# A hybrid MLA and RWKV-7 layer with a PEER mixture on one core: which token blocks go through every expert and which gather, and 32 expert tiles' first products moved beside the mixers

## The chip, the cores and the metric

The kernel runs on one core of a Trainium2 chip. The metric is the device time of one execution in microseconds (us), lower is better. The engines are PE (TensorE; PEld is its weight load, which overlaps the matmuls), DVE (VectorE), ACT (ScalarE), POOL (GpSimd) and SP (SyncE, which issues most of the DMAs). Each engine works off its own instructions in a fixed order.

## The reference

512 tokens, model width 1024, all float32. Two mixers read the normed tokens, and a product-key expert layer follows. Cut to its core:

```python
h = rms_norm(x, g_mix);  p = h @ w_in
y_a = mla_group(p[..., :672], ...)      # latent attention, 8 heads, causal by chunks of 64
y_b = rwkv7_group(p[..., 672:], ...)    # RWKV-7, 8 heads, a state carried over the tokens
x = x + concat([y_a, y_b]) @ w_o
# PEER on h = rms_norm(x, g_ffn), 16384 experts of one neuron each
q = (h @ w_pq).reshape(T, 8, 2, 128)
s = einsum('thpd,hpnd->thpn', q, sub_keys)           # 128 scores per half key
s1, i1 = top_k(s[:, :, 0], 16);  s2, i2 = top_k(s[:, :, 1], 16)
top_s, pos = top_k(s1[..., :, None] + s2[..., None, :], 16)
idx = take(i1 * 128 + i2, pos);  gate = softmax(top_s)   # 8 heads x 16 = 128 experts a token
act = gelu(einsum('thkd,td->thk', expert_u[idx], h))
x = x + einsum('thk,thkd->td', gate * act, expert_v[idx])
```

## The kernel before

The tokens are four blocks of 128 (block 0 to 3). Work on them is written as generators that run in lanes: `front` (norm and the input columns of RWKV), `chunks` (RWKV within chunks), `latent` (the whole attention group), `scan` (RWKV's state), and one lane `back`, which holds the output projection, the second norm, the retrieval (queries against keys, top 16) and the routing (indices and gates). A loop at the end of the kernel picks the lane that is furthest behind in a table of costs; a scheduler of the framework then fixes the order of each engine's instructions. Lanes have pools of their own for SBUF and PSUM; the back lane has two PSUM banks.

The expert layer is done in two ways:

- **Gathered blocks** (`GATHERED`, `experts`): POOL fetches for each of the 128 (head, rank) pairs the rows of `expert_u` that the 128 tokens want, 128x1024 float32 by an indirect DMA into a tile `ga` (four buffers). DVE takes the product with the block's `h2` (one SCALAR_TENSOR_TENSOR and a read of its accumulator). The rows of `expert_v` are fetched likewise and added into `acc` by a second SCALAR_TENSOR_TENSOR. A block is 256 gathers of 512 KB, two blocks are 512. They can begin when the block's routing has written `idx`.
- **Dense blocks** (`DENSE`, `dense`): two blocks go through all 16384 experts, in 128 tiles of 128 experts. `gate_half` spreads the two blocks' gates over the experts (DVE makes B, ACT makes A, PE multiplies). `up(e)` multiplies a tile of `expert_ut` with the tokens: whole in float32, or split into two float32r halves by ACT and DVE (`split`) and three cheaper products on PE. `down(e)` multiplies the result with the gates on DVE and then with a tile of `expert_v`, whole or split, into four PSUM banks `po`. `u_whole` and `v_split` say which tile is done how. A few tiles' results (`KEPT`) are made early and wait in DRAM.

Before, block 0 and block 3 are gathered, and blocks 1 and 2 are dense; the back lane takes block 0 alone, then 1 and 2 together, then 3.

Of the kernel before, what the change touches and what calls it, by code (L numbers as in the profile page):

```python
# [8 lines left out]
F32 = mybir.dt.float32  # L9
# [47 lines left out]

LANE = {"R": 1, "M": 2, "S": 4, "F": 3, "B": 3}
# [4 lines left out]
PM = 7  # L63
BACK = [("F", (0,)), ("F", (1,)), ("B", (0,)), ("B", (1, 2)), ("B", (3,))]

GATHERED = (0, 3)
DENSE = (1, 2)
EARLY = 1
GROUP, GA = 32, 4


HALF, SUB, GBUFS = 64, 16, 5
FIRST, AHEAD, KEPT = 12, 16, 12
VB, SPB, XB, UCUT = 2, 2, 4, 2
# [3 lines left out]
def u_whole(e):  # L78

    return e < 28 or 47 <= e - AHEAD < 64  # L80

# [6 lines left out]
def layer_kernel(ctx: ExitStack, tc: tile.TileContext, x, pos, cvec, rvec, w_mla, w_rwkv, w_uq, w_ukv, lora, g2,  # L88
# [46 lines left out]
    def cst(shape, name, dt=F32, pool=pre):  # L135
        return pool.tile(shape, dt, name=name)
# [200 lines left out]
    def rwkv_in(b, hT):  # L337
        pm = {}
        if b == EARLY:

            t = [gb([P, D], "ga", GA).rearrange("p (a b) -> p a b", b=P) for _ in range(2)]
            pm = {"k": t[0][:, 0:4], "r": t[0][:, 4:8], "v": t[1][:, 0:4], "x": t[1][:, 4:6]}
        for g, cols in (("x", (12, 13)), ("k", range(4, 8)), ("r", range(4)), ("v", range(8, 12))):
            if b != EARLY:
                pm[g] = sb([P, 4, P], "pm", PM, pool=wa) if len(cols) == 4 else sb([P, 2, P], "px", 2, pool=wa)
# [508 lines left out]
    def route(b, tv, ti):  # L854
# [100 lines left out]
        o = DENSE.index(b) * P  # L955
        if not slots:
            slots.extend(pools[2].tile([P, nd], F32, tag="vs_2", name=f"slots{j}", bufs=3) for j in range(3))
        for j, dst in enumerate(slots):
            act(dst[:, o:o + P], p[:, j * P:(j + 1) * P], AF.Copy)

# [49 lines left out]

    def back(bs):
# [4 lines left out]
        lists = yield from retrieve(bs, h2T)  # L1016
        for b, (tv, ti) in zip(bs, lists):
            routed[b] = yield from route(b, tv, ti)

    def gate_half(dn, g, parts):  # L1020
# [23 lines left out]
    def dense():  # L1044
# [13 lines left out]
        def halves(shape, tag, bufs, pool=None, one=False):  # L1058
            cnt[0] += 1
            return [(pool or d2).tile(shape, F32R, tag=tag if one else tag + n, name=f"{tag}{n}{cnt[0]}", bufs=bufs)  # L1060
                for n in "hl"]

        hd = []
        for i in range(0, KC, 2):
# [15 lines left out]

        kept = {}
# [64 lines left out]
        n = nd // 8  # L1146
        rest = AHEAD - FIRST + KEPT
        for e in range(FIRST):
            up(e)
        for i, _ in enumerate(gate_half(dn, 0, [whole])):  # L1150
            for e in range(FIRST + i * rest // n, FIRST + (i + 1) * rest // n):
                up(e, e >= AHEAD)
        po = [[psd.tile([P, 512], F32, tag="po", name=f"po{i}{n}", bufs=2 * nt) for n in range(2)] for i in range(nt)]
# [26 lines left out]
    after = {"F": lambda b: [("R", b - 2), ("F", b - 1)] + ([("S", 0)] if b == 1 else []),  # L1180
             "R": lambda b: [("F", b)], "M": lambda b: [("F", b)],
             "S": lambda b: [("R", b)], "B": lambda b: [("S", b), ("M", b)]}
    lanes = [[("R", (b,)) for b in range(NB)], [("M", (b,)) for b in range(NB)], [("S", (b,)) for b in range(NB)],
             [(n, bs) for n, bs in BACK], [("F", (b,)) for b in range(2, NB)]]

# [3 lines left out]
    while any(lanes):  # L1189
# [15 lines left out]
        if running[i] is None:  # L1205
            running[i] = fn(bs) if n == "B" else fn(*bs)
            at[i] = t
# [71 lines left out]
```

## Time and profile before

| | |
|---|---|
| Median of 3 runs | 1789.32 us (1785.22 to 1790.51) |
| The profiled execution | 1786.83 us, of which its instructions span 1784.9 us |
| Busy share of the span | PE 91%, PE weight loads 76%, DVE 76%, ACT 51%, POOL 41% |
| Mean granted TensorE clock | 0.942 of full speed |
| Moved by DMA | 520.84 MB, a mean of 292 GB/s |

A busy share is the share of the span in which at least one instruction of the engine ran. Matmuls are pipelined, so that the busy share of PE counts their latency too. A difference of more than about 0.3% of the time can be told from none.

### The profile page before, as it was taken

The page shows a single profiled execution, that of the slowest core. Times are in us where ns is not written, and L with a number is a line of the kernel's source. Part 1 is how long each engine was busy: PE and PEld are TensorE (multiplying, and loading weights), DVE is VectorE, ACT ScalarE, POOL GpSimd, SP SyncE. Part 2 cuts the span into 40 slices and gives each one's busy share as a digit, 9 for nine tenths or more (in the row PEclk, how much of TensorE's full clock was granted, in tenths as well). Part 3 has the DMA queues.
Part 4 walks back from the last instruction along what each step waited for, and adds up shares of the span by engine and source line. Part 5 has one row for each costly group of instructions (what it writes and reads, how often), then busy time and mean ns, then how long its engine had stood idle before and what let it go on. Part 6 is the DMA issues. An engine that isn't in the chain of part 4 may idle for free. (4 is left out here: it accounts for less than half of the span.)

```text
span 1784.9 us, 31084 instructions
## 1 busy us (share of the span) xinstructions
PE 1622.3 (91%) x11143; PEld 1363.3 (76%) x11143; DVE 1352.8 (76%) x3010; ACT 907.3 (51%) x2421; POOL 723.1 (41%) x560
## 2 busy tenths in 40 slices
PE   7999998998879995789997799999989889999998
PEld 6896898877665784667995478888867778888876
DVE  3422446667775698987889789999878799999895
ACT  5645635444422622257766234444777735444444
POOL 1001100447664433555445343544555554447430
PEclk9999997995769998998998999999989999999999
DMA  8545643898789998889997799999889889999985
GB/s 276 187 139 191 237 163 111 322 313 268 262 272 329 318 313 305 287 297 331 376 328 244 284 363 355 330 348 340 313 318 324 310 306 355 373 340 333 354 280 177
DMA packets 154875, 520.84 MB, mean 292 GB/s; under 512 B 17313, under 2 KB 24097, under 8 KB 154721
## 3 DMA queue, kind: packets, MB, share of 16 engines
q0 software_dynamic: 73728, 268.47, 43.1%
q1 hardware_dynamic: 80992, 250.39, 39.3%
q8 instruction: 88, 1.44, 0.3%
q14 instruction: 67, 0.54, 0.1%
HBM read 508.96 MB, written 9.83 MB: 291 GB/s over the span
## 5 line engine op out<-in xcount | busy, mean ns | idle before, releaser
L970 POOL DMA_INDIRECT ga<-in_expert_v_dram,idx x256 | 359.0, 1402 | 366.7 <-DVE acc L983 260.9
L970 POOL DMA_INDIRECT ga<-in_expert_u_dram,idx x256 | 311.9, 1218 | 337.7 <-DVE ga L980 234.2
L983 DVE SCALAR_TENSOR_TENSOR acc<-ga,dots,acc 128x1024 f32<-128x1024 f32 x256 | 327.6, 1280 | 63.7 <-DMA ga<-in_expert_v_dram,idx 60.8
L980 DVE SCALAR_TENSOR_TENSOR ga<-ga,h 128x1024 f32<-128x1024 f32 x256 | 311.6, 1219 | 65.0 <-DMA ga<-in_expert_u_dram,idx 62.1
L1141 PE MATMUL po<-xh,t 128*128 128x512 f32 x880 | 305.2, 406 | 11.7 <-DVE t L1056 5.6
L1109 PE MATMUL ps<-dh,ul 128*128 128x256 f32 x664 | 192.7, 290 | 10.6 <-DVE ul L1056 10.0
L1055 ACT ACTIVATE xh<-v 128x512 fp32r<-128x512 f32 x220 | 136.4, 627 | 121.5 <-PE po L1141 99.7
L1109 PE MATMUL ps<-dh,uh 128*128 128x256 f32 x664 | 189.7, 286 | 6.7 <-ACT uh L1055 5.2
L1141 PEld LDWEIGHTS po<-xh,t 128*128 128x128 f32 x880 | 160.9, 192 | 44.4 <-DVE t L1056 6.8
L1141 PE MATMUL po<-xl,t 128*128 128x512 f32 x440 | 179.2, 408 | 11.1 <-DVE xl L1056 10.4
L1109 PE MATMUL ps<-dl,uh 128*128 128x256 f32 x664 | 188.7, 284 | 0.0
L1095 PE MATMUL ps<-t,u 128*128 128x256 f32 x720 | 172.5, 392 | 12.8 <-DMA u<-in_expert_ut_dram 11.1
L1056 DVE TENSOR_TENSOR xl<-v,xh 128x512 fp32r<-128x512 f32 x220 | 149.6, 688 | 36.6 <-ACT xh L1055 34.1
L1095 PEld LDWEIGHTS ps<-t,u 128*128 128x128 f32 x720 | 138.6, 197 | 36.8 <-issue 6.6
L1031 ACT ACTIVATE A<-iotap,slots 128x128 f32<-128x128 f32 x512 | 156.2, 394 | 0.0
L1035 PEld LDWEIGHTS ps<-B,A 128*128 128x128 f32 x1024 | 128.8, 200 | 23.2 <-ACT A L1032 11.9
L1109 PEld LDWEIGHTS ps<-dh,ul 128*128 128x128 f32 x664 | 127.3, 192 | 21.8 <-DVE ul L1056 16.5
L1055 ACT ACTIVATE uh<-u 128x512 fp32r<-128x512 f32 x166 | 99.7, 626 | 86.3 <-PE ps L1109 67.6
L1109 PEld LDWEIGHTS ps<-dh,uh 128*128 128x128 f32 x664 | 127.4, 192 | 16.7 <-ACT uh L1055 8.0
L1035 PE MATMUL ps<-B,A 128*128 128x64 f32 x1024 | 128.5, 281 | 10.6 <-ACT A L1032 9.4
L1109 PEld LDWEIGHTS ps<-dl,uh 128*128 128x128 f32 x664 | 127.3, 192 | 3.0 <-issue 0.2
L840 PE MATMUL ps<-h2T,wst 128*128 128x128 f32 (+1 forms) x768 | 123.5, 315 | 1.6 <-DMA wst<-in_w_pq_dram 1.6
(391 smaller groups left out, 2845.7 us busy)
## 6 DMA issues: line engine op xcount, KB each, us to landing
u<-in_expert_ut_dram SPq DMA_DIRECT2D x128, 512.0 KB
v<-in_expert_v_dram SPq DMA_DIRECT2D x128, 512.0 KB
wst<-in_w_rwkv_dram SPq DMA_DIRECT2D x56, 512.0 KB
wst<-in_w_pq_dram SPq DMA_DIRECT2D x48, 512.0 KB
wst<-in_w_o_dram SPq DMA_DIRECT2D x24, 512.0 KB
wst<-in_w_mla_dram SPq DMA_DIRECT2D x16, 336.0 KB
t<-in_x_dram SPq DMA_DIRECT2D x8, 512.0 KB
wst<-in_w_ukv_dram SPq DMA_DIRECT2D x16, 256.0 KB
```

What stands on the lines that cost most here:

```text
L840: mm(p[:, :nb * P], w[:, kc, :], h2T[:, kc, :], start=kc == 0, stop=kc == KC - 1)
L970: G.indirect_dma_start(out=t, out_offset=None, in_=table, in_offset=bass.IndirectOffsetOnAxis(ap=idx[:, j:j + 1], axis=0))
L980: V.scalar_tensor_tensor(u, u, 1.0, h2, op0=OP.mult, op1=OP.mult, accum_out=dots[:, j:j + 1])
L983: V.scalar_tensor_tensor(acc, row_of(expert_v, j), dots[:, j:j + 1], acc, op0=OP.mult, op1=OP.add)
L1031: act(A[:, j, :], iotap, AF.Abs, scale=-1.0, bias=i2T[:, t0 + j:t0 + j + 1])
L1035: mm(p[:, j * HALF:(j + 1) * HALF], A[:, j, :], B[:, j, :], start=True, stop=True)
L1055: act(hi, t, AF.Copy)
L1056: V.tensor_tensor(lo, t, hi, op=OP.subtract)
L1095: mm(p, u[:, kc, :], hd[kc // 2][:, kc % 2, :], start=kc == 0, stop=kc == KC - 1)
L1109: mm(p, a[:, k, :], h[:, kc, :], start=kc + i == 0, stop=kc == KC - 1 and i == 2)
L1141: mm(po[i][n], ww[:, i * P:(i + 1) * P], vv, start=e + k == 0, stop=e == P - 1 and k == 2)
```

## The change

Blocks 0 and 1 become the dense pair, blocks 2 and 3 are gathered. The back lane is cut in two steps, `join` (output projection and norm) and `query` (retrieval and routing), and takes 0 and 1 together, then 2, then 3. A new lane `beside` starts when blocks 0 and 1 are joined: it reads their normed tokens back from DRAM, multiplies the first 32 tiles of `expert_ut` with them, whole, and writes the 32 results to DRAM; its PSUM is the back lane's two banks. `up(e)` of these tiles later loads the result and applies the gelu alone. Of the tiles after those, 16 instead of 12 are made ahead and kept in DRAM, and `u_whole` now holds for e < 48, so that 20 tiles fewer are split. The indices and gates of the dense blocks wait in DRAM (`slotd`). Tiles for the inputs of RWKV are shared with the `ga` buffers in two blocks instead of one.

```diff
-BACK = [("F", (0,)), ("F", (1,)), ("B", (0,)), ("B", (1, 2)), ("B", (3,))]
-
-GATHERED = (0, 3)
-DENSE = (1, 2)
-EARLY = 1
+PM = 3
+BACK = [("F", (0,)), ("F", (1,)), ("N", (0, 1)), ("Q", (0, 1)), ("N", (2,)), ("Q", (2,)), ("N", (3,)), ("Q", (3,))]
+
+GATHERED = (2, 3)
+DENSE = (0, 1)
+
+EARLY = (1, 2)
+
+BESIDE = 32
...
-FIRST, AHEAD, KEPT = 12, 16, 12
+FIRST, AHEAD, KEPT = 12, 16, 16
...
-    return e < 28 or 47 <= e - AHEAD < 64
+    return e < BESIDE + KEPT or 47 <= e - AHEAD < 64
...
+    def beside(_):
+
+        hd = ux.tile([P, KC, nd], F32, name="hdx")
+        nc.sync.dma_start(hd, h2d)
+        for e in range(BESIDE):
+            u = ux.tile([P, KC, P], F32, tag="ux", name=f"ux{e}", bufs=2)
+            nc.sync.dma_start(u, expert_ut[e])
+            p = bank()[:, :nd]
+            for kc in range(KC):
+                mm(p, u[:, kc, :], hd[:, kc, :], start=kc == 0, stop=kc == KC - 1)
+            t = ux.tile([P, nd], F32, tag="uy", name=f"uy{e}", bufs=2)
+            act(t, p, AF.Copy)
+            kept[e] = dp.tile([P, nd], F32, name=f"a{e}")
+            nc.sync.dma_start(kept[e], t)
+            yield
...
             if e in kept:
                 acts[e] = act_tile(e)
                 nc.sync.dma_start(acts[e], kept[e])
+                if e < BESIDE:
+                    act(acts[e], acts[e], AF.Gelu)
                 return
...
     stages = {"F": (front, 16, 32), "R": (chunks, 24, 110), "M": (latent, 46, 95), "S": (scan, 10, 28),
-              "B": (back, 42, 95)}
...
+              "N": (join, 11, 28), "Q": (query, 31, 67), "U": (beside, BESIDE, 8 * BESIDE)}
```

**Where the gathers begin.** On DVE, before, the first product of a gathered row (L980) stands at row 376 of 2062, among the mixers of blocks 2 and 3:

```order
L583 TENSOR_TENSOR pm_1792<-pm_1792,t_3862 128x512
L597 TENSOR_TENSOR pm_1915<-pm_1915,pm_1792 128x512
L980 SCALAR_TENSOR_TENSOR ga_15350,dots_15349<-ga_15350,h_15347 128x1024
L577 TENSOR_TENSOR t_3675<-t_3675,ps_3786 128x512
L353 SCALAR_TENSOR_TENSOR px_3479<-ps_3528,cv,px_3479 128x128
L353 SCALAR_TENSOR_TENSOR pm_3545<-ps_3548,cv,pm_3545 128x128
L748 TENSOR_TENSOR ST_164<-t_3794,ps_3789 64x4x64 x2
```

Of the change the first one (now L984) stands at row 688 of 1971, behind the routing of block 2 (L922):

```order
L922 SCALAR_TENSOR_TENSOR t_6677<-pi_6620,dl_6566 128x128 x7
L953 TENSOR_TENSOR gate_6810<-ge_6804,gs_6807 128x128
L922 SCALAR_TENSOR_TENSOR t_6677<-pi_6620,dl_6566 128x128 x2
L922 SCALAR_TENSOR_TENSOR t_6677<-bf_6695,dl_6566 128x128 x16
L984 SCALAR_TENSOR_TENSOR ga_15054,dots_15053<-ga_15054,h_15051 128x1024
L984 SCALAR_TENSOR_TENSOR ga_15057,dots_15053<-ga_15057,h_15051 128x1024
```

Before, 169 of the 512 products stand ahead of the dense stage's first DVE instruction; now 42 do, and none of the 512 stands ahead of an instruction of RWKV or attention.

**Where they end.** Before, the last products of gathered rows (L983) stand among the splits of the last dense tiles (L1056), and the row of the dense output (L1173) is last on DVE:

```order
L1056 TENSOR_TENSOR xl_14936<-v_14919,xh_14935 128x512
L983 SCALAR_TENSOR_TENSOR acc_16127<-ga_16902,dots_16131,acc_16127 128x1024
L1056 TENSOR_TENSOR t_15052<-wst_14293,t_15052 128x256
L1056 TENSOR_TENSOR xl_14952<-v_14945,xh_14951 128x512
L983 SCALAR_TENSOR_TENSOR acc_16127<-ga_16905,dots_16131,acc_16127 128x1024
L1056 TENSOR_TENSOR xl_14962<-v_14945,xh_14961 128x512
...
L1056 TENSOR_TENSOR xl_15326<-v_15309,xh_15325 128x512
L1173 TENSOR_TENSOR xx_15335<-xx_15335,po_8318 128x512
```

Of the change the last split (now L1081) stands at row 1861, and 102 products of gathered rows (L984, L987) stand behind it:

```order
L1081 TENSOR_TENSOR xl_15020<-v_15013,xh_15019 128x512
L1081 TENSOR_TENSOR xl_15030<-v_15013,xh_15029 128x512
L984 SCALAR_TENSOR_TENSOR ga_16302,dots_15835<-ga_16302,h_15833 128x1024
L1202 TENSOR_TENSOR xx_15039<-xx_15039,po_8706 128x512
L1202 TENSOR_TENSOR xx_15039<-xx_15039,po_8707 128x512
L987 SCALAR_TENSOR_TENSOR acc_15831<-ga_16305,dots_15835,acc_15831 128x1024
...
L987 SCALAR_TENSOR_TENSOR acc_15831<-ga_16537,dots_15835,acc_15831 128x1024
```

The gathers moved from both sides of the dense stage's start to its whole length and past its end.

**Where the 32 tiles stand.** On PE, before, the queries of blocks 1 and 2 (L840, against `w_pq`) stand between matmuls of block 3's attention (L482 to L499):

```order
L493 MATMUL ps_5136<-ident,t_5086 128x128 x4
L840 MATMUL ps_5984<-h2T_5293,wst_5982 128x256 x8
L499 MATMUL ps_5157<-vs_5073,t_5141 128x64
...
L840 MATMUL ps_6017<-h2T_5293,wst_6015 128x256 x6
L493 MATMUL ps_5210<-ident,t_5128 128x128 x4
```

Of the change the queries of block 2 (now L845) stand between tiles of `beside` (L1038) and the last steps of the scan (L727 to L778):

```order
L845 MATMUL ps_6118<-h2T_5840,wst_6116 128x128 x8
L1038 MATMUL ps_6130<-hdx,ux_6128 128x256 x8
L727 MATMUL ps_6926<-t_6924,t_6801 64x64 x3
...
L1038 MATMUL ps_6408<-hdx,ux_6406 128x256 x8
L845 MATMUL ps_6423<-h2T_5840,wst_6421 128x128 x8
L778 MATMUL ps_7004<-sg_5688,wst_7002 128x128
```

Behind the last query matmul of block 2 no attention is left; 19 of the 32 tiles stand ahead of that matmul, 24 ahead of the end of block 2's routing.

## Rows read from the trace of the kernel before

**Rows 1.** The page's first part: engine, busy us, share of the span, instructions.

```profile
PE 1622.3 (91%) x11143; PEld 1363.3 (76%) x11143; DVE 1352.8 (76%) x3010; ACT 907.3 (51%) x2421; POOL 723.1 (41%) x560
```

**Rows 2.** The chain that ended last, its longest piece: start, us, what.

```profile
1737.32 37.45 PE po L1141 x159
```

**Rows 3.** Four stretches: us; PE, PEld, DVE, ACT, POOL busy; granted clock; DMA share; GB/s.

```profile
0.00:319.00 319.00, 299.67 (x2895) 256.51 (x2896) 127.68 (x548) 172.40 (x554) 23.82 (x29) 0.97 0.56 185
319.00:700.00 381.00, 337.84 (x2589) 275.97 (x2587) 280.77 (x609) 155.52 (x496) 199.68 (x168) 0.87 0.88 305
700.00:1010.00 310.00, 259.04 (x1508) 216.95 (x1509) 270.73 (x812) 173.95 (x452) 149.19 (x111) 0.91 0.86 303
1010.00:1738.00 728.00, 685.96 (x3987) 582.27 (x3986) 649.39 (x1004) 385.58 (x884) 350.45 (x255) 0.98 0.93 334
```

**Rows 4.** Single lines: durations ns min/median/max, first and last start in us.

```profile
L952 ACT ACTIVATE idx<-ps x2: 278/278/278, 318.2 to 1004.4; 128x128 int32<-128x128 f32 x2
L840 PE MATMUL ps<-h2T,wst x256: 274/275/377, 213.2 to 279.1; 128*128 128x128 f32 x128
L840 PE MATMUL ps<-h2T,wst x256: 377/379/483, 603.0 to 691.5; 128*128 128x256 f32 x128
L840 PE MATMUL ps<-h2T,wst x256: 273/275/423, 844.8 to 928.8; 128*128 128x128 f32 x128
L499 PE MATMUL ps<-t,t x64: 221/275/421, 85.0 to 697.5; 128*128 128x64 f32 x64
```

**Rows 5.** PE by time, 859 to 864 us: one whole tile, and what follows it.

```profile
859.69 3.67 PE L1095 MATMUL ps<-t,u 128*128 128x256 f32 x16
863.20 0.38 PE L847 MATMUL ps<-wst,t 128*128 128x128 f32 x2
```

**Rows 6.** Groups of instructions: busy us, mean ns of one, then idle time before.

```profile
L983 DVE SCALAR_TENSOR_TENSOR acc<-ga,dots,acc 128x1024 f32<-128x1024 f32 x256 | 327.6, 1280 | 63.7 <-DMA ga<-in_expert_v_dram,idx 60.8 <-issue 1.3 <-DVE dots L987 0.6
L1056 DVE TENSOR_TENSOR xl<-v,xh 128x512 fp32r<-128x512 f32 x220 | 149.6, 688 | 36.6 <-ACT xh L1055 34.1 <-PE po L1141 2.2
L1056 DVE TENSOR_TENSOR ul<-u,uh 128x512 fp32r<-128x512 f32 x166 | 110.0, 688 | 9.0 <-ACT uh L1055 7.8 <-PE ps L1109 0.7
L1056 DVE TENSOR_TENSOR t<-wst,t 128x256 fp32r<-128x256 f32 x36 | 15.1, 421 | 0.0
L1126 DVE TENSOR_TENSOR wst<-wst,G 128x256 f32<-128x256 f32 x42 | 24.9, 605 | 3.6 <-ACT wst L1117 3.5
L1027 DVE TENSOR_TENSOR B<-iotap,slots 128x512 f32<-128x512 f32 x64 | 42.9, 685 | 6.6 <-PE ps L1035 6.4
L821 DVE FIND_INDEX8 ti<-tv,t 128x8 uint32<-128x128 f32 x64 | 17.5, 284 | 0.0
```

**Rows 7.** DVE by time, instructions back to back: start, us, what.

```profile
449.35 1.23 DVE L980 SCALAR_TENSOR_TENSOR ga<-ga,h 128x1024 f32<-128x1024 f32 x1
450.50 0.08 DVE L980 DVE_READ_ACCUMULATOR ga<-ga,h 128x1 f32 x1
450.60 1.28 DVE L983 SCALAR_TENSOR_TENSOR acc<-ga,dots,acc 128x1024 f32<-128x1024 f32 x1
...
468.55 0.68 DVE L577 TENSOR_TENSOR t<-t,ps 128x512 f32<-128x512 f32 x1
469.15 0.68 DVE L760 TENSOR_TENSOR t<-t,gnr 128x512 f32<-128x512 f32 x1
```

**Rows 8.** DMA: the gathers' queue, the queue of SP, and GB/s by slice.

```profile
GB/s 276 187 139 191 237 163 111 322 313 268 262 272 329 318 313 305 287 297 331 376 328 244 284 363 355 330 348 340 313 318 324 310 306 355 373 340 333 354 280 177
...
q0 software_dynamic: 73728, 268.47, 43.1%
q1 hardware_dynamic: 80992, 250.39, 39.3%
```

**Rows 9.** POOL by time: the first and the last of twelve gathers in their fastest stretch.

```profile
401.02 1.98 POOL L970 DMA_INDIRECT ga<-in_expert_u_dram,idx  x1 [0.68 <-DVE ga L980]
...
421.85 0.94 POOL L970 DMA_INDIRECT ga<-in_expert_v_dram,idx  x1 [0.97 <-DVE acc L983]
```

More of the change, by code (lines that the diff above doesn't have):

```diff
@@ L55 @@
 NCAND = sum(n for _, n in RUNS)
-LANE = {"R": 1, "M": 2, "S": 4, "F": 3, "B": 3}
+LANE = {"R": 1, "M": 2, "S": 4, "F": 3, "N": 3, "Q": 3, "U": 3}
 BANKS = {1: 4, 2: 2, 3: 2}
@@ L62 @@
 WST = {4: (1, RW), 1: (1, RW), 2: (2, H * QK), 3: (3, D)}
-PM = 7
-BACK = [("F", (0,)), ("F", (1,)), ("B", (0,)), ("B", (1, 2)), ("B", (3,))]
-GATHERED = (0, 3)
-DENSE = (1, 2)
-EARLY = 1
+PM = 3
[4 more added lines that the diff above has]
+BESIDE = 32
 GROUP, GA = 32, 4
 HALF, SUB, GBUFS = 64, 16, 5
-FIRST, AHEAD, KEPT = 12, 16, 12
+FIRST, AHEAD, KEPT = 12, 16, 16
 VB, SPB, XB, UCUT = 2, 2, 4, 2
@@ L105, in layer_kernel @@
     wa = early.enter_context(tc.tile_pool(name="wa", bufs=1))
+    ux = early.enter_context(tc.tile_pool(name="ux", bufs=1))
     for n in (1, 4):
@@ L251, in layer_kernel @@
     h2d = dp.tile([P, KC, nd], F32, name="h2d")
+    slotd = dp.tile([P, 3, nd], F32, name="slotd")
     identb = cst([P, P], "identb", BF16, pool=con)
@@ L338, in rwkv_in @@
         pm = {}
-        if b == EARLY:
+        if b in EARLY:
             t = [gb([P, D], "ga", GA).rearrange("p (a b) -> p a b", b=P) for _ in range(2)]
@@ L343, in rwkv_in @@
         for g, cols in (("x", (12, 13)), ("k", range(4, 8)), ("r", range(4)), ("v", range(8, 12))):
-            if b != EARLY:
-                pm[g] = sb([P, 4, P], "pm", PM, pool=wa) if len(cols) == 4 else sb([P, 2, P], "px", 2, pool=wa)
+            if b not in EARLY:
+                pm[g] = sb([P, 4, P], "pm", PM, pool=wa) if len(cols) == 4 else sb([P, 2, P], "px", 1, pool=wa)
             for i, c in enumerate(cols):
@@ L955, in route @@
         o = DENSE.index(b) * P
[L956 to L959, printed above, removed]
+        t = med(3, P)
+        act(t, p[:, :3 * P].rearrange("p (a b) -> p a b", a=3), AF.Copy)
+        nc.sync.dma_start(slotd[:, :, o:o + P], t)
     def experts(b, idx, gate):
@@ L1009, in scan, with join @@
         yield from rwkv_scan(b, *parts.pop(b), yTs[b])
-    def back(bs):
+    def join(*bs):
         xts = yield from out_proj(bs, [yTs.pop(b) for b in bs])
@@ L1015, in back, with query @@
             yield from norm_ffn(b, xt, h2T[:, :, i * P:(i + 1) * P])
-        lists = yield from retrieve(bs, h2T)
+        parts[bs] = h2T
+    def query(*bs):
+        lists = yield from retrieve(bs, parts.pop(bs))
         for b, (tv, ti) in zip(bs, lists):
             routed[b] = yield from route(b, tv, ti)
+    kept = {}
+    def beside(_):
[12 more added lines that the diff above has]
+            yield
     def gate_half(dn, g, parts):
@@ L1061, in halves @@
                 for n in "hl"]
+        for j in range(3):
+            slots.append(pools[2].tile([P, nd], F32, tag="vs_2", name=f"slots{j}", bufs=3))
+            nc.sync.dma_start(slots[j], slotd[:, j, :])
         hd = []
@@ L1079, in act_tile @@
             return taken[0][:, i * nd:(i + 1) * nd]
-        kept = {}
         def up(e, keep=False):
@@ L1146, in dense @@
         n = nd // 8
-        rest = AHEAD - FIRST + KEPT
         for e in range(FIRST):
@@ L1150, in dense @@
         for i, _ in enumerate(gate_half(dn, 0, [whole])):
-            for e in range(FIRST + i * rest // n, FIRST + (i + 1) * rest // n):
-                up(e, e >= AHEAD)
+            for e in range(FIRST + i * (AHEAD - FIRST) // n, FIRST + (i + 1) * (AHEAD - FIRST) // n):
+                up(e)
+            for e in range(i * KEPT // n, (i + 1) * KEPT // n):
+                up(BESIDE + e, True)
         po = [[psd.tile([P, 512], F32, tag="po", name=f"po{i}{n}", bufs=2 * nt) for n in range(2)] for i in range(nt)]
@@ L1178, in layer_kernel @@
     stages = {"F": (front, 16, 32), "R": (chunks, 24, 110), "M": (latent, 46, 95), "S": (scan, 10, 28),
-              "B": (back, 42, 95)}
-    after = {"F": lambda b: [("R", b - 2), ("F", b - 1)] + ([("S", 0)] if b == 1 else []),
+              "N": (join, 11, 28), "Q": (query, 31, 67), "U": (beside, BESIDE, 8 * BESIDE)}
+    after = {"F": lambda b: [("R", b - 2), ("F", b - 1)],
              "R": lambda b: [("F", b)], "M": lambda b: [("F", b)],
-             "S": lambda b: [("R", b)], "B": lambda b: [("S", b), ("M", b)]}
+             "S": lambda b: [("R", b)], "N": lambda b: [("S", b), ("M", b)], "Q": lambda b: [("N", b)],
+             "U": lambda b: [("N", b)]}
     lanes = [[("R", (b,)) for b in range(NB)], [("M", (b,)) for b in range(NB)], [("S", (b,)) for b in range(NB)],
-             [(n, bs) for n, bs in BACK], [("F", (b,)) for b in range(2, NB)]]
+             [(n, bs) for n, bs in BACK], [("F", (b,)) for b in range(2, NB)],
+             [("U", DENSE[-1:])]]
     done = {}
@@ L1205, in layer_kernel @@
         if running[i] is None:
-            running[i] = fn(bs) if n == "B" else fn(*bs)
+            running[i] = fn(*bs)
             at[i] = t
```

## The prediction

> **What bounds the kernel now.** I read the page's busy shares first, then the chain that ended last, then four stretches of the span, since the work changes along it. By the page PE is the busiest engine, 91% of the span [rows 1], and the chain ends in a run of 37 us of the second products, in which nothing else holds the kernel up [rows 2]. The reader is to see in the stretches why that average misleads. Up to 319 us, when the first gathered block's indices are ready [rows 4], PE is busy 94% of the time and DVE 40%, and the DMA engines 56%. From 319 to 700 us the mixers of blocks 2 and 3 share the core with gathers: 168 POOL instructions, nearly all of them gathers, DVE at 74%, DMA at 88%, while PE's granted clock falls to 0.87. From 1010 us to 1738 us the dense stage and the second block's gathers fill three resources together: PE 94%, DVE 89%, DMA 93% [rows 3]. So in the late stretch no engine has room to take over much, and the room is early: DVE is idle for 191 us and the DMA engines for some 140 us of the first 319 us (0.44 times 319).
>
> The Trainium skill (Perfetto Trace Analysis, Identifying the Most-Contended Engine) says that matmul busy time is a poor measure of how near TensorE is to its limit, and that the share of weight loads is a better one. Here that share is 76%, as large as DVE's [rows 1]. By the matmul share the 32 tiles taken off the late stretch are the gain; by the other measure DVE and DMA decide, and to them the change gives little. That is the first rival below against my sum, which stands on the rows alone.
>
> **The change part by part.** A mark that both programs share makes the sum simple: the last query matmul of the first three blocks. Before, it starts at 691.5 us, and attention's last matmul at 697.5 us [rows 4]. At that point of the changed PE order the same mixers and the same 256 query matmuls are done, plus 19 whole tiles. By then the gathers have not begun.
>
> *The mark in the changed kernel.* A whole tile takes 3.51 us of PE at full clock, from one start to the next [rows 5], so 19 tiles are 67 us. What can hide them: PE is idle 19 us up to 319 us and 43 us from there to 700 us, and 338 busy us at a clock of 0.87 are 294 us at full clock, 44 us less [rows 3]; 106 us in all. If all of it takes tiles, the mark even comes a little earlier, at 697 + 67 - 106 = 658 us; if none, at 764 us. The gathers' products (1.2 us each, in DVE's order among the mixers' small steps) go, which shortens the mixers' chains; on the other hand blocks 2's norm and queries now stand behind block 3's attention, so a chain of short steps lies at the end. I take 45 us of the 106: 719 us.
>
> *Block 2's routing.* From the last query matmul to the indices block 0 took 39 us (279.1 to 318.2) with the core to itself, and block 3 took 76 us (928.8 to 1004.4) among gathers and dense tiles [rows 4]. Without gathers it is nearer the first; tiles of beside share the lane's two banks, so I take 42 us. The first gather starts at about 761 us instead of 319 us; the ends are 697 (658 + 39) and 840 (764 + 76).
>
> *DVE after that.* All 512 products and every DVE instruction of the dense stage stand behind this point. DVE's instructions overlap a little: a product of 1.23 us and its read are followed after 1.25 us, and an instruction of 0.68 us over 512 columns after 0.60 us [rows 7], so I take 0.08 us off each duration. 256 pairs of products are 256 x (1.25 + 1.20) = 627 us; 350 splits of 512 columns (390 before, less 40 for 20 tiles no longer split) at 0.61 = 214 us; 110 of 256 columns at 0.34 = 37 us; 128 products with gates at 0.52 = 67 us; 128 for B at 0.60 = 77 us [rows 6]; the 165 or so instructions of block 3's retrieval and routing at 0.2 us, 33 us (0.284 less 0.08). Sum 1055 us.
>
> *DMA after that.* The gathers' 268.47 MB took 43.1% of 1784.9 us, 769 us of all 16 engines, 1.50 us for each gather; SP's queue took 701 us for 250.39 MB, 2.80 us for 1 MB [rows 8]. Behind the first gather SP still loads 128 tiles of v, 96 of u and 8 of beside (121.6 MB), moves 64 kept tiles of 0.131 MB (8.4 MB), and block 3's weights and the blocks' rows, some 13 MB: 143 MB, 400 us. Sum 1170 us at these prices; at the best slice, 376 GB/s [rows 8], 412 MB are 1096 us. PE has some 900 us left and ACT less, so they are covered.
>
> The Trainium skill (DMA: Bandwidth & Descriptors, Where 436 GB/s comes from) puts the ceiling of a core's 16 DMA engines at 435 GB/s; 412 MB would then be 947 us, and DVE's sum would stand alone. The trace does not bear it out, with 376 GB/s in its best slice; the rival that would follow is the second below.
>
> *The tail.* In DVE's order 102 products stand behind the last split. With the dense work over, a gather costs at least its 1.50 us of DMA. The fastest stretch of the trace needs 20.83 us for 11 gathers, 1.89 us each [rows 9], with mixers beside it, and the four buffers stay as they are. I take 1.75 us: 178 us (153 to 193). Before, the tail was PE's 37 us.
>
> *The stretch between.* Ahead of the tail lie 1055 - 102 x 1.23 = 930 us of DVE and 1170 - 153 = 1017 us of DMA. In 1010 to 1738 us these two ran at 89% and 93% [rows 3], which gives 1045 and 1094 us. PE, at 94% then, has less to do now, so a little more can be had of both: 1050 us (at least 955, for 359 MB at 376 GB/s; at most 1120).
>
> *Sum.* 761 + 1050 + 178 + 4 for the last product and its store = 1993 us of span. The profiled execution took 1.9 us beyond its span, and the median of the runs stands 2.5 us above it; I round to 1992 us. What the change gives, 32 tiles off the late PE, is not in the sum, because PE is not what the late stretch then waits for. What it costs is seen in one figure: 168 early POOL instructions, about 150 gathers, with 150 x 1.23 = 185 us of DVE and 225 us of DMA, move from beside the mixers into the full stretch, and the mixers leave DVE and DMA idle.
>
> **The rivals.**
> - *PE is the bound (faster).* The late stretch is 94% PE [rows 3], and 32 tiles at 3.51 us are 112 us. If the gathers ended in time, the span would shrink by that less what the early stretch can't hide, about 22 us: 1695 us. For it the gathers must begin 1050 + 178 + 4 us before 1785, at 553 us, but PE's work ahead of that point is 585 us at full clock (291 + 294, rows 3) before any tile. Against it stands that row; I give it 0.03, and 0.02 that the gains and losses meet within 0.3%.
> - *The two resources pack tightly (slower by less).* All of PE's spare time takes tiles, first gather at 697 us, and DMA runs at its best slice throughout with no tail to speak of: 697 + 1096 + 4 = 1797 us as the least, and 1797 to 1885 us with a tail of 1.5 us a gather and some waits. For it: slices of 0.97 and more exist [rows 8]. By the skill's ceiling DMA would not count, and from 761 us DVE's 1055 us would end at 1820 us. 0.15.
> - *The beside lane holds up block 2 (slower by more).* Its tiles share two PSUM banks with the queries, and each stands between two of them in PE's order. If each of the 13 tiles from block 2's queries to its indices delays the chain by its 3.5 us and an eviction, and nothing of the 67 us is hidden, gathers begin at 840 us: 2075 us, up to 2130 us with a slow stretch between. 0.12.
> - *The forecast*, 1885 to 2075 us: 0.68.
>
> **How the numbers follow.** The time is the forecast's, 1992 us. The forecast's ends come from 697 and 840 us for the first gather and 955 to 1120 us for the stretch between, which won't all fall on one side. The range 1875 to 2080 us leaves out the far half of the tight rival and most of the beside rival. Faster by over 0.3% 0.03, within 0.3% (what this kernel's measurement can't tell from no change) 0.02, slower 0.95.
>
> **What would show it.** In the changed profile: the first gather at 700 to 840 us; DVE below 40% busy up to then, and PE at a granted clock of 0.95 or more from 319 us on; DMA share 0.9 or more and DVE 0.87 or more from there to the last split, PE below 0.9; then 150 to 195 us in which POOL, DMA and DVE work on gathers alone, with PE idle, and a chain that ends in gathers and their products instead of po. I am wrong if the gathers start before 600 us, if the tail is short because the gathers keep up with the dense tiles, or if DMA moves much more than 376 GB/s.

## The result, and the profile after

The changed kernel takes 2045.38 us (median of 4 runs, 2043.16 to 2050.02); the kernel before, run beside it, 1787.27 us. The ratio is 1.1449, with a 95% interval of 1.1414 to 1.1485: 14% slower. 1992 us were forecast, in a range of 1875 to 2080 us: the time lies in the range, 53 us above the forecast. The profiled execution's span is 2044.9 us.

The page of the changed kernel: its first part, two lines of the 40 slices, and the chain that ended last with its shares by engine and by line.

```profile
PE 1670.4 (82%) x10983; PEld 1375.6 (67%) x10983; DVE 1335.9 (65%) x2970; ACT 894.2 (44%) x2407; POOL 709.8 (35%) x560
...
PE   7999999999999987788887689988899999980000
...
PEclk9999999899879988888887989998999999995555
...
PE 45%; DMA 21%; issue 12%; DVE 10%; POOL 7%; ACT 4%; SPq 0%; POOLq 0%; DVEq 0%; ACTq 0%
```

Against [rows 1] DVE falls from 76% to 65% of the span with nearly the same busy time: the work is the same and the span has holes. The last four slices show one, with no PE work at all (and PE's granted clock at 0.5, the level of 1.2 GHz, with PE idle; it costs nothing there). Three single lines place the parts, as [rows 4] did.

```profile
L957 ACT ACTIVATE idx<-ps x2: 267/272/277, 753.3 to 978.2; 128x128 int32<-128x128 f32 x2
L845 PE MATMUL ps<-h2T,wst x256: 273/276/377, 659.2 to 720.0; 128*128 128x128 f32 x128
L1081 DVE TENSOR_TENSOR xl<-v,xh x26: 683/687/743, 1799.8 to 1843.8; 128x512 fp32r<-128x512 f32 x26
```

Block 2's last query matmul starts at 720.0 us, the indices are written at 753.3 us (319 us in the kernel before), and the last split of the dense stage stands at 1843.8 us. Cut at these points, and at 1039 us where the first second product of the dense stage runs, the stretches are (columns as in [rows 3]):

```profile
0.00:754.00 754.00, 716.68 (x5954) 594.52 (x5955) 279.23 (x1223) 346.64 (x1104) 47.34 (x48) 0.95 0.49 156
754.00:1039.00 285.00, 234.91 (x1295) 204.32 (x1294) 220.09 (x517) 158.98 (x415) 143.37 (x120) 0.85 0.90 321
1039.00:1844.00 805.00, 716.78 (x3732) 575.40 (x3730) 704.77 (x1088) 388.13 (x887) 397.37 (x295) 0.95 0.93 334
1844.00:2041.00 197.00, 2.08 (x8) 1.38 (x8) 131.46 (x144) 0.46 (x2) 121.76 (x99) 0.51 0.82 274
754.00:1844.00 1090.00, 951.69 (x5024) 779.72 (x5022) 924.86 (x1604) 547.11 (x1301) 540.74 (x415) 0.93 0.92 330
```

Read the first row against the last but one. For 754 us DVE is 37% busy and the DMA engines 49%, because no gather can run yet. For the last 197 us only gathers run, at 99 POOL instructions, 2.0 us each. In that tail nothing is full: DMA 0.82, DVE 67%. DVE and POOL by time show why (start, us, what, and the idle time before with what ended it):

```profile
1886.81 1.28 DVE L987 SCALAR_TENSOR_TENSOR acc<-ga,dots,acc 128x1024 f32<-128x1024 f32 x1 [1.24 <-DMA ga<-in_expert_v_dram,idx]
1888.37 0.94 POOL L974 DMA_INDIRECT ga<-in_expert_v_dram,idx  x1 [0.75 <-DVE acc L987]
1889.34 1.23 DVE L984 SCALAR_TENSOR_TENSOR ga<-ga,h 128x1024 f32<-128x1024 f32 x1 [1.25 <-DMA ga<-in_expert_u_dram,idx]
...
1890.84 0.93 POOL L974 DMA_INDIRECT ga<-in_expert_u_dram,idx  x1 [1.54 <-DVE ga L984]
```

POOL waits for a product to free a buffer, and DVE waits for a gather to land: a ring of four buffers. Experiment 3 tests it.

### The profile page after: what moved, and what is told of

Read it like the earlier page. It is cut to its first block, busy times and chain, and to the rows that moved or that the text cites. A ratio compares the mean times of both kernels' runs of the same rounds, so it can differ in the third digit from the quotient of the medians.

```text
span 2044.9 us, 30921 instructions
## 1 busy us (share of the span) xinstructions
PE 1670.4 (82%) x10983; PEld 1375.6 (67%) x10983; DVE 1335.9 (65%) x2970; ACT 894.2 (44%) x2407; POOL 709.8 (35%) x560
## 4 chain that ended last, share of the span: by engine, by line
PE 45%; DMA 21%; issue 12%; DVE 10%; POOL 7%; ACT 4%; SPq 0%; POOLq 0%; DVEq 0%; ACTq 0%
DMA ga<-in_expert_v_dram,idx 10%; PE po L1169 7%; POOL ga L974 7%; DMA ga<-in_expert_u_dram,idx 6%; PE ps L1137 6%; PE ps L355 5%; PE ps L1038 4%; PE ps L845 4%; PE ps L671 4%; PE ps L789 3%; DVE ga L984 2%; DVE acc L987 2%; DMA v<-in_expert_v_dram 2%; PE ps L487 1%; PE ps L504 1%
## 5 line engine op out<-in xcount | busy, mean ns | idle before, releaser
L974 POOL DMA_INDIRECT ga<-in_expert_u_dram,idx x256 | 297.9, 1164 | 342.9 <-DVE ga L984 237.1
L987 DVE SCALAR_TENSOR_TENSOR acc<-ga,dots,acc 128x1024 f32<-128x1024 f32 x256 | 328.4, 1283 | 83.5 <-DMA ga<-in_expert_v_dram,idx 81.5
L984 DVE SCALAR_TENSOR_TENSOR ga<-ga,h 128x1024 f32<-128x1024 f32 x256 | 312.5, 1223 | 104.7 <-DMA ga<-in_expert_u_dram,idx 103.9
L1169 PE MATMUL po<-xh,t 128*128 128x512 f32 x880 | 315.4, 417 | 27.3 <-ACT xh L1080 18.2
L1081 DVE TENSOR_TENSOR xl<-v,xh 128x512 fp32r<-128x512 f32 x220 | 147.9, 689 | 21.7 <-ACT xh L1080 21.2
L1060 PEld LDWEIGHTS ps<-B,A 128*128 128x128 f32 x1024 | 133.9, 210 | 34.0 <-ACT A L1057 22.3
L1056 ACT ACTIVATE A<-iotap,slots 128x128 f32<-128x128 f32 x512 | 156.2, 394 | 0.0
L1060 PE MATMUL ps<-B,A 128*128 128x64 f32 x1024 | 135.2, 294 | 22.1 <-ACT A L1057 18.2
L1137 PE MATMUL ps<-dh,ul 128*128 128x256 f32 x504 | 145.5, 289 | 7.5 <-DVE ul L1081 7.2
L1137 PE MATMUL ps<-dh,uh 128*128 128x256 f32 x504 | 144.2, 286 | 3.3 <-ACT uh L1080 3.2
L1137 PE MATMUL ps<-dl,uh 128*128 128x256 f32 x504 | 143.8, 285 | 0.0
L845 PE MATMUL ps<-h2T,wst 128*128 128x128 f32 (+1 forms) x768 | 129.9, 327 | 13.7 <-DMA wst<-in_w_pq_dram 13.6
L1123 PE MATMUL ps<-t,u 128*128 128x256 f32 x528 | 136.6, 414 | 0.2 <-ACT G L1065 0.2
L845 PEld LDWEIGHTS ps<-h2T,wst 128*128 128x128 f32 x768 | 113.7, 203 | 23.3 <-issue 8.7
L1169 PEld LDWEIGHTS po<-xl,t 128*128 128x128 f32 x440 | 86.5, 197 | 56.9 <-DVE xl L1081 40.2
L1038 PE MATMUL ps<-hdx,ux 128*128 128x256 f32 x512 | 124.4, 395 | 0.1
L1123 PEld LDWEIGHTS ps<-t,u 128*128 128x128 f32 x528 | 108.1, 210 | 18.3 <-issue 1.6
```

Of the source, the lines that this page charges most:

```text
L845: mm(p[:, :nb * P], w[:, kc, :], h2T[:, kc, :], start=kc == 0, stop=kc == KC - 1)
L974: G.indirect_dma_start(out=t, out_offset=None, in_=table, in_offset=bass.IndirectOffsetOnAxis(ap=idx[:, j:j + 1], axis=0))
L984: V.scalar_tensor_tensor(u, u, 1.0, h2, op0=OP.mult, op1=OP.mult, accum_out=dots[:, j:j + 1])
L987: V.scalar_tensor_tensor(acc, row_of(expert_v, j), dots[:, j:j + 1], acc, op0=OP.mult, op1=OP.add)
L1038: mm(p, u[:, kc, :], hd[:, kc, :], start=kc == 0, stop=kc == KC - 1)
L1056: act(A[:, j, :], iotap, AF.Abs, scale=-1.0, bias=i2T[:, t0 + j:t0 + j + 1])
```

## The experiments

**1. The gathers' start moved, by no other edit.** If the early gathers are what the change loses, the kernel before should lose as much when only their start is moved. Block 0's indices are kept as floats, and made integers only when a later result is there: block 1's routing, or (in the milder version) block 1's normed input.

```diff
+            if b == 0:
+                act(idx.bitcast(F32), p[:, :P], AF.Copy)
+                held.append(idx)
+                return idx, gate
...
+    def let_go(late):
+        z = gb([P, 1], "z")
+        V.tensor_scalar(z, late, 0.0, None, op0=OP.mult)
+        idx = held.pop()
+        act(idx, idx.bitcast(F32), AF.Identity, bias=z)
...
+            if b == 1:
+                let_go(slots[0][:, 0:1])
```

> The kernel before, all in place, but block 0's gathers wait: its index list is turned into integers only once block 1's routing has been written (about 757 us there, 753.8 us is the change's first gather). No products beside the mixers, no new pairing of blocks. If what the change costs is the gathers that no longer run beside the mixers (150 of them before 700, some 170 before 758, and the change lost about 255 us: 1.5 us each), this kernel loses about as much: 1980 to 2050 us, and its end is gathers alone, as 146 of their products stand behind the last dense row. If the loss came from the new pairing, the beside products or their waits in DRAM, the time stays at 1785 to 1850.

> The same, held only until block 1's normed input of the experts is there (597 us in the kernel before). Some 110 of the 170 early gathers are lost. At 1.5 us each that is 165 us: 1900 to 1970 us, between the kernel before and the one held to 758. If it is a matter of the order at the end alone (71 gather products behind the last dense row here, 146 there, 0 before), about half of the other's loss; if the early gathers are worth nothing, 1785 to 1810.

Measured: 1986.94 us for the later hold (ratio 1.1096, 1.1049 to 1.1143) and 1876.36 us for the milder one (1.0486, 1.0454 to 1.0517). The first is inside what was expected; the second is below its 1900, because without gathers the mixers run faster and both holds end earlier than the kernel before suggests. The stretches, of the later hold and then of the milder one:

```profile
319.00:665.00 346.00, 335.05 (x2787) 271.37 (x2786) 145.65 (x655) 165.77 (x523) 24.23 (x20) 0.98 0.38 124
870.00:1701.00 831.00, 772.09 (x4264) 638.20 (x4264) 734.76 (x1156) 414.74 (x938) 395.73 (x291) 0.96 0.92 331
1701.00:1980.00 279.00, 0.36 (x1) 0.00 (x0) 183.98 (x206) 0.46 (x2) 172.44 (x141) 0.51 0.82 273
```

```profile
909.00:1735.00 826.00, 772.26 (x4280) 634.83 (x4280) 734.99 (x1172) 414.78 (x939) 396.69 (x288) 0.97 0.92 331
1735.00:1869.00 134.00, 0.01 (x1) 0.00 (x0) 90.26 (x94) 0.23 (x1) 81.05 (x67) 0.52 0.81 274
```

And two rows of the kernel before: the time of the first row above, and the same dense stage, from its first second product to the last product of a gathered row:

```profile
319.00:665.00 346.00, 308.27 (x2405) 249.76 (x2404) 251.28 (x508) 144.02 (x462) 186.34 (x155) 0.86 0.87 302
964.00:1735.00 771.00, 719.26 (x4102) 600.26 (x4102) 687.20 (x1095) 394.43 (x901) 373.00 (x263) 0.98 0.91 329
```

The reader is to see two things. Up to 665 us PE's granted clock is 0.98 with no gathers beside it, where the kernel before had 0.86 over the same time: the mixers gain from the gathers' absence, and yet the kernel loses. And the dense stage takes 771 to 831 us in all three and carries 263 to 291 gathers. Gathers that it does not carry, and that were not done before it, are left for the end at 2.0 us each (279 us for 141, 134 for 67).

How many are left was fixed before the run, in the order of DVE's instructions. The expectations counted 146 and 71 products behind the last dense row there; the traces have 146 and 71 behind the last split (of the later hold, the products behind it):

```profile
L995 DVE SCALAR_TENSOR_TENSOR acc<-ga,dots,acc x89: 1279/1285/1287, 1701.1 to 1978.9; 128x1024 f32<-128x1024 f32 x89
L992 DVE SCALAR_TENSOR_TENSOR ga<-ga,h x57: 1218/1226/1297, 1698.2 to 1915.9; 128x1024 f32<-128x1024 f32 x57
```

So the holds move the order at the end along with the gathers' start. The milder one lost 0.44 of what the later one lost (88 of 199 us), and the products left over (71 of 146, 0.49) fit that no worse than the early gathers lost (77 of 137, 0.56): the two readings were not told apart. How many gathers the dense stage would carry in another order wasn't tried.

The first gathers at 504.5 and 665.8 us instead of 319.3 made the spans 1873.2 and 1984.3 instead of 1784.9. The kernel before issues 77 and 137 gathers up to those times, so a lost early gather costs 88/77 = 1.15 and 199/137 = 1.45 us; in the change, with 170 up to 753.8 us, 260/170 = 1.53. The first ones may cost less because the kernel before ends with 37 us of PE alone [rows 2], under which late gathers first hide; no run tests that.

**2. The change without the products beside the mixers.** Same blocks, same order, but the 32 tiles go back to the dense stage, with 12 tiles kept in DRAM and 20 more tiles split, as before.

```diff
-FIRST, AHEAD, KEPT = 12, 16, 16
+FIRST, AHEAD, KEPT = 12, 16, 12
...
-    return e < BESIDE + KEPT or 47 <= e - AHEAD < 64
+    return e < 28 or 47 <= e - AHEAD < 64
...
-                up(BESIDE + e, True)
+                up(AHEAD + e, True)
...
-             [("U", DENSE[-1:])]]
+             ]
```

> The change without the lane beside the mixers: blocks 0 and 1 dense, 2 and 3 gathered, no tile made early, 20 more tiles split, 12 kept as before. My theory (the late start of the gathers costs, not the lane): the first gather comes some 55 us earlier, at about 700 us, the late stretch has 112 us more of PE and 24 us more of DVE, and DVE's order has 126 products behind the last split instead of 102, 240 us of tail at 1.9 us each; in all 2010 to 2070 us, about that of the change. Rival, the lane itself costs: 1980 us or less. Rival, the lane's relief of PE carries the late stretch: 2120 us or more.

Measured: 2007.35 us (1.1247, 1.1194 to 1.1301), just under the range of my theory, and 38 us faster than the whole change (the two were timed apart). So what the tiles take from the dense stage is worth less than what they cost:

```profile
714.00:942.00 228.00, 186.33 (x1142) 169.30 (x1140) 183.97 (x468) 147.35 (x383) 112.35 (x96) 0.84 0.88 309
942.00:1755.00 813.00, 763.62 (x4240) 630.66 (x4240) 730.16 (x1133) 413.82 (x945) 395.93 (x295) 0.97 0.94 341
1755.00:1993.00 238.00, 0.23 (x1) 0.00 (x0) 160.19 (x179) 0.46 (x2) 144.92 (x122) 0.51 0.81 278
```

In the dense stage the change has 47 us less of PE (716.78 for 763.62) and finishes it 8 us sooner (805 for 813) with the same 295 POOL instructions. PE is not what that stage waits for. In return the first gather comes 40 us later (753.8 for 713.5), and the dense stage starts 97 us later (1039 for 942). The gate tiles' first matmul shows the second delay (line L1060 here, and the beside tiles' line in the change; first and last start are the times after the durations):

```profile
L1060 PE MATMUL ps<-B,A x752: 218/275/477, 722.2 to 1298.2; 128*128 128x64 f32 x188
```

```profile
L1060 PE MATMUL ps<-B,A x512: 219/276/474, 869.4 to 1028.8; 128*128 128x64 f32 x171
L1038 PEld LDWEIGHTS ps<-hdx,ux x512: 186/190/338, 379.6 to 851.2; 128*128 128x128 f32 x171
```

The gates begin at 869.4 us, 18 us behind the last beside tile (851.2 us), and at 722.2 us without that lane. The lane's buffers lie in a pool whose memory the dense stage takes over, which would explain it. The fixed order of PE's instructions, in which queries of block 3 run between the two, could as well. Neither was tried apart.

**3. The gathers alone.** The dense stage is left out (and with it the outputs of blocks 0 and 1), once with four gather buffers and once with six.

```diff
-    dense()
```

```diff
-GROUP, GA = 32, 4
+GROUP, GA = 32, 6
...
-            u = ux.tile([P, KC, P], F32, tag="ux", name=f"ux{e}", bufs=2)
+            u = ux.tile([P, KC, P], F32, tag="ux", name=f"ux{e}", bufs=1)
...
-            t = ux.tile([P, nd], F32, tag="uy", name=f"uy{e}", bufs=2)
+            t = ux.tile([P, nd], F32, tag="uy", name=f"uy{e}", bufs=1)
```

The six buffers are paid for by one buffer each for the beside tiles' input and output; the first gather comes at 757.8 us all the same (753.4 with four).

> The change without the dense stage: the outputs of blocks 0 and 1 are left out. What stays behind 754 us is the gathers and block 3's routing. My theory (four buffers' turnaround): 512 gathers at 1.85 to 1.9 us, 1700 to 1740 us. Rival, DMA sets a gather's price, 1.5 us: 1525 us; rival, DVE does, 1.23 us: 1390 us.

> The gathers-only kernel (the stage of dense work, and with it the output of blocks 0 and 1, left out; span 1774.7 us, 512 gathers in some 1017 us, 1.9 us each) with six gather buffers for four. Its 1.9 us a gather lies under no engine's limit: DVE was busy 65% and DMA 81% of 1000 to 1700. If the pace is the turn of four buffers (issue, 5.6 us to landing, product), six make it about 1.5 us, where the 4 KB rows of 128 partitions fill the DMA engines (about 270 MB at some 355 GB/s): 770 us of gathers, an end at about 1550 to 1610 us. If the pace is GpSimd's own (0.93 to 2 us of descriptors a gather), the end stays at 1740 to 1780.

Measured, one run each: 1776.89 us with four buffers, 37 us above the 1740 of the buffer theory but far from its rivals, and 1574.73 with six, inside its range.

```profile
1000.00:1700.00 700.00, 0.00 (x0) 0.00 (x0) 456.28 (x551) 1.15 (x5) 449.95 (x365) 0.50 0.81 275
```

```profile
1000.00:1500.00 500.00, 0.00 (x0) 0.00 (x0) 418.88 (x513) 1.15 (x5) 389.85 (x339) 0.50 0.97 358
```

With nothing beside them the gathers take 700/365 = 1.92 us each through four buffers and 500/339 = 1.47 us through six, where the DMA engines are full at 0.97 and 358 GB/s. So in the change the gathers, once they start at 754 us, cannot end much before 1775 us through four buffers: almost the whole time of the kernel before, with the dense stage not yet counted.

**4. Which of two resources fills the late stretch.** In one run each product on a gathered row covers 512 of 1024 columns on DVE (the other half is left out), with whole transfers; in the other the transfers bring 512 columns (the other half of each row left out, the first half used twice) and DVE's instructions keep their length.

```diff
-                    V.scalar_tensor_tensor(u, u, 1.0, h2, op0=OP.mult, op1=OP.mult, accum_out=dots[:, j:j + 1])
+                    V.scalar_tensor_tensor(u[:, :512], u[:, :512], 1.0, h2[:, :512], op0=OP.mult, op1=OP.mult, accum_out=dots[:, j:j + 1])
```

```diff
-            G.indirect_dma_start(out=t, out_offset=None, in_=table,
+            G.indirect_dma_start(out=t[:, :512], out_offset=None, in_=table.rearrange("n (a d) -> (n a) d", a=2),
```

> The change with each gathered row's product taken over 512 of its 1024 columns on VectorE (the other half of each dot product and sum is left out); the transfers stay whole. It takes some 0.55 us from each of 1024 products on a gathered row, about 560 us of VectorE's time over the kernel, all of it behind 754 us. If DMA fills the late stretch first, as forecast (DMA 0.9 or more there), the time falls only to where DMA ends, 754 + 1170 = 1924 and what is left of a tail: 1900 to 1990 us. If VectorE sets the late stretch: 1750 to 1880. If TensorE does (the rival): 2000 to 2050, no change.

> The change with 512 of 1024 columns fetched for each gathered row (the other half of each row is left out, the first half taken twice), so that VectorE's instructions keep their length and count while the gathers' bytes are halved, 268 to 134 MB per table pair. If DMA sets the late stretch: it ends where VectorE's work ends, 754 + 1055 = 1809, and some of the tail: 1800 to 1900 us. If VectorE sets it: 1960 to 2050. If TensorE does: 2000 to 2050, no change.

Measured: 1972.98 us with half of DVE's work on gathers (1.1039, 1.0959 to 1.1118) and 1938.69 us with half of their bytes (1.0844, 1.0767 to 1.0920). The first is as forecast; the second lies between the two theories' figures and so decides for neither alone. The dense stage of each, to be set against the row from 1039 to 1844 us above:

```profile
1039.00:1808.00 769.00, 707.43 (x3748) 575.65 (x3747) 558.92 (x1090) 387.46 (x887) 336.71 (x294) 0.96 0.95 350
```

```profile
1026.00:1783.00 757.00, 699.17 (x3738) 565.43 (x3736) 704.11 (x1091) 394.00 (x887) 429.91 (x297) 0.97 0.76 253
```

With DVE relieved to 73% the DMA engines fill up to 0.95; with DMA relieved to 0.76 DVE stands at 93%. Either stays near its limit when the other is eased, so the stage shortens by only 36 or 48 us of 805. PE is 92% busy in both, so a third limit is not far off. The rest of the gain is the tail, 160 and 153 us instead of 197, and with half of the bytes a dense stage that starts 13 us sooner. Neither relief gives back more than 107 us of the 258 that the change cost. Nor could it take the tail away: 95 and 97 products stand behind the last split there, 102 in the change, since the order of the instructions stayed nearly as it was.

**5. The tail, five buffers and the gate tiles.** Five gather buffers should let the gathers keep up. They fit only if the gate tiles A have one buffer instead of two (and, in the change, the beside tiles' output one).

```diff
-GROUP, GA = 32, 4
+GROUP, GA = 32, 5
...
-            A = dn.tile([P, 8, P], F32, tag="A", name=f"A{g}_{t0}", bufs=2)
+            A = dn.tile([P, 8, P], F32, tag="A", name=f"A{g}_{t0}", bufs=1)
```

> The change with five gather buffers instead of four, paid for by one buffer less for A in the gates and one less in the lane beside the mixers. The order of DVE then has no product behind the last split (102 before) and 142 instructions of the dense stage behind the last product. My theory (the tail and the pace of 1.89 us a gather come from four buffers' turnaround, about 7.5 us each): the tail goes and PE or DMA ends the kernel, 1940 to 2000 us. Rival, a gather's pace is that of the DMA engines or of POOL: the gathers run late against the order, DVE waits for them, and the time stays at 2030 to 2060 us.

> The kernel before with five gather buffers for four, and one buffer for the gate tiles of the dense stage. If the early stretch's pace of gathers (1.9 us each at its fastest, with DVE at 0.6) is the turn of four buffers, gathers run ahead earlier and the late stretch has less left: 1720 to 1770 us. If the dense stage then lacks cover or the pace is DVE's, as in the change with five buffers, where the end did not move: 1775 to 1800.

Both missed. The change with five buffers took 2047.67 us (1.1468, 1.1414 to 1.1521), no faster, which is the rival's range but, as the controls show, not its reason; its last product of a gathered row came at 1896 us, but PE then worked on alone for 145 us, to the end. The kernel before with five took 1940.06 us (1.0880, 1.0790 to 1.0971). I had read the first as a tail that only changes its owner. The two controls, with the one gate buffer alone and four gather buffers, show what I had overlooked:

```diff
-            A = dn.tile([P, 8, P], F32, tag="A", name=f"A{g}_{t0}", bufs=2)
+            A = dn.tile([P, 8, P], F32, tag="A", name=f"A{g}_{t0}", bufs=1)
```

> The change with one buffer for four gather-stage neighbours' gate tiles in place of two, and nothing else (four gather buffers). The order then stands otherwise: no gather product behind the last dense row (102 in the change) and 46 dense rows behind the last gather product (142 in the version with five buffers, which was no faster). If the tail of gathers alone (197 us at 1.9 us each) is time in which dense work could have run, a balanced end gives it back in part: from the two measured mixes (754 to 1844 with 410 gathers and all dense work, and 754 to 1896 with 512 gathers and 0.85 of it) about 1980, so 1960 to 2010 us. If the late stretch is full by its sum whatever the order: 2030 to 2060.

> The kernel before with one buffer for the gate tiles in place of two, and four gather buffers as there. In the order, 351 dense rows then stand behind the last gather product (39 before, 365 with five gather buffers and one gate buffer, which took 1940 us). If that order is why five buffers were slower, this one is slow as well: 1890 to 1960 us, with a stretch at the end in which TensorE is full and no gather runs. If the five buffers themselves were the cause: 1780 to 1810.

The change with that alone took 2091.57 us (1.1686, 1.1651 to 1.1721), against my 1960 to 2010; the kernel before 1961.90 us (one run), 2 us above the 1890 to 1960 expected. So the single gate buffer costs 46 and some 174 us by itself, and five gather buffers (with the beside tiles' one output buffer, in the change) give back 44 and some 22. Of the change with one gate buffer, by line: the gate stage's matmuls, and what PE waited for ahead of them (us, times), for which the same view of the change has the second line; then the stretch.

```profile
L1060 PE MATMUL ps<-B,A x512: 219/421/477, 870.3 to 1155.0; 128*128 128x64 f32 x171
...
  ACT A L1057: 196.0, 36
```

```profile
  ACT A L1057: 30.7, 18
```

```profile
754.00:1166.00 412.00, 266.01 (x1281) 230.35 (x1281) 297.80 (x611) 162.20 (x408) 232.96 (x183) 0.75 0.87 303
```

With one buffer PE waits 196 us for gate tiles, where the change waits 31 us, and the dense stage begins at 1166 us instead of 1039. The order is skewed too: gathers get ahead, and dense work is left for the end, when PE is alone. In the kernel before with one gate buffer that end is 340 us long:

```profile
1613.00:1953.00 340.00, 335.59 (x1996) 297.86 (x1995) 206.49 (x354) 181.29 (x360) 0.00 (x0) 0.98 0.54 174
```

A tail of either kind is lost time. How much a balanced end would give the change was not shown: no version tried has one.

**6. The other way round: blocks 0 and 1 gather.** The kernel before with blocks 0 and 1 gathered and 2 and 3 dense, so that both gathered blocks start early.

```diff
-BACK = [("F", (0,)), ("F", (1,)), ("B", (0,)), ("B", (1, 2)), ("B", (3,))]
+BACK = [("F", (0,)), ("F", (1,)), ("B", (0,)), ("B", (1,)), ("B", (2, 3))]
...
-GATHERED = (0, 3)
-DENSE = (1, 2)
+GATHERED = (0, 1)
+DENSE = (2, 3)
```

> The kernel before with blocks 0 and 1 gathered, blocks 2 and 3 dense, the back lane taking 0, 1 and then 2 and 3 together: the gathers as early as can be, the dense stage later. My theory (idle DVE and DMA beside the mixers is what counts): gathers from 319 us on without a gap, all done by some 1400 us, the last stretch bound by PE alone; 1690 to 1790 us. Rival, PE bounds the late stretch and where the gathers lie does not matter: the dense stage starts some 70 us later, since both its blocks are routed last, 1830 to 1880 us.

Measured: 1891.96 us (1.0604, 1.0529 to 1.0679), against my 1690 to 1790, and 12 us above the rival's 1880. Early gathers are not enough: the routing of the dense blocks is now last, and the dense stage's first second product runs at 1094.8 us for 965.1.

```profile
1094.00:1665.00 571.00, 528.42 (x2906) 434.31 (x2905) 498.79 (x757) 298.95 (x709) 291.50 (x209) 0.97 0.92 332
1665.00:1886.00 221.00, 220.54 (x1323) 196.17 (x1322) 141.31 (x236) 116.86 (x226) 0.66 (x1) 1.00 0.55 187
```

Its tail is 221 us of PE alone, with the gathers done: the mirror image of the change.

## Why the prediction was right

**The mark**, block 2's last query matmul, was forecast at 719 us and is 720.0 us. That 45 of 106 us of spare time would take the tiles was chosen, not derived, so that it came within 1 us is luck. Experiment 2 shows where the 45 came from. Without the lane the same matmul starts at 667.1 us (the last start in this row):

```profile
L845 PE MATMUL ps<-h2T,wst x256: 272/275/377, 609.6 to 667.1; 128*128 128x128 f32 x128
```

Some 9.5 us of the dense stage's own tiles run ahead of it there. So the lane's 67 us of tiles moved the mark by 53 us, or some 62 with those, and hid little; about 39 of the 45 us are mixers that run faster without gathers (697 us before, 667 less 9.5 there). One sign I had named failed: PE's granted clock is 0.92 from 319 to 720 us and 0.85 from there to 754, not 0.95 or more, though without the lane it is 0.96 up to 713 us. The third rival (the lane holds up block 2) had a real mechanism, but it needed gathers at 840 us or later.

**Block 2's routing** took 33 us (720.0 to 753.3) where 42 were forecast (46 without the lane, 667.1 to 712.9); the first gather is at 753.8 us for 761.

**DVE and DMA after that.** DVE's work from 754 to 2041 us is 924.9 + 131.5 = 1056 us, forecast 1055; DMA's 0.92 x 1090 + 0.82 x 197 = 1164 us, forecast 1170. The sum of durations held.

**The stretch between** was sized at 1050 us and took 1090 (754 to 1844). The step that was off is the share: I took DVE's 89% and DMA's 93% from a stretch in which the dense stage runs from end to end. From 1039 us on the change has 88% and 0.93. But for 285 us ahead of that, with block 3's queries and the gates, DVE is at 77% and DMA at 0.90. That the dense stage would start 75 us later than before (1039 for 964) was in no step of mine; experiment 2 shows that it is gone without the lane (942).

**The tail** was sized at 1.75 us a gather, 178 us, and took 197 (1844 to 2041). I had allowed for less than 1.89 because no mixers are beside the gathers. Experiment 3 showed that the four buffers set the pace, not the neighbours: 1.92 us alone, and 1.47 with six.

These four differences, -7, +40, +19 and next to nothing at the end, are the 52 us between 1993 and the span of 2044.9 us.

**PE isn't what the late stretch waits for**: shown by experiment 2 for the dense stage, where 47 us less of PE bought 8. The first rival (faster, 1695 us) needed gathers from 553 us on, and they came at 754. The Trainium skill (Perfetto Trace Analysis, Identifying the Most-Contended Engine) would have the share of weight loads tell more than matmul busy time. Here both fell with the longer span, 67% and 82%, and neither names the bound; the experiments did.

**The tight packing** (1797 to 1885 us) failed on the start and on the pace: DMA at 0.92 and 330 GB/s on the mean of the stretch. The longest full stretch of any run is 358 GB/s at a share of 0.97 (500 us of gathers alone, six buffers). The Trainium skill (DMA: Bandwidth & Descriptors, Where 436 GB/s comes from) has, beside the ceiling of 435 GB/s that the prediction weighed, about 358 GB/s as what HBM gives one core. I had passed that figure over. An estimate by that figure of the Trainium skill is 1151 us for the 412 MB, which lifts the rival's least time from 1797 to 1852 us, still inside its range. The long stretches here agree with the figure, but three slices of 39 us of the six-buffer run reach 398 to 412 GB/s, so it is no ceiling here.

**The signs.** DVE was 37% busy up to the first gather (below 40 forecast), PE 87% from there to the last split (below 90), and then 197 us of gathers alone with PE idle (150 to 195). DMA's 0.92 there is above the 0.9 named, DVE's 85% below the 0.87. The chain ends in gathers: from 1844 us on, their landings are 58% of it, and PE has no part.

**The cause**, then, is the one forecast: gathers that used to run beside the mixers. Experiment 1 shows it with no other edit, at 199 us for a start at 665.8 us; what part of that is the order at the end, which moves with the start, stays open. The change starts its gathers 88 us later still, of which the lane is 40; the rest of that delay, from the new order of blocks, was not taken apart.

## What to carry to other kernels

When a stream of transfers can run beside work that doesn't need its engines, count what of it is done before the full stage begins: here that stage took 771 to 831 us and carried 263 to 295 POOL instructions in five kernels, and each gather left over cost 2 us at the end. Count also what the instruction order leaves for the end: the products behind the last split could be counted before the run, and easing an engine hardly changed them. Moving load off the busiest engine gains nothing if it delays the start of such a stream or of the next stage. Change one buffer count at a time: five buffers looked useless until the one that had been given up for them was tried alone.

## What the runs showed of the hardware

Gathers alone, through four buffers, leave DMA at 0.81 and DVE at 65% and yet take 1.92 us each, so neither engine's share says that the ring is full; six buffers bring 1.47 us with DMA at 0.97. And PE runs the mixers at a granted clock of 0.98 without gathers beside them (319 to 665 us) and at 0.86 with them, over the same time. So the early stretch isn't free for the gathers, only cheaper.
